# A hybrid attention and DeltaNet layer: the first triangular solve moved from VectorE to GpSimd, its closing operations pinned, and four more PSUM banks for the convolutions ahead of it

## The chip, the cores and the metric

The kernel runs on one core of a Trainium2 chip. The core has TensorE (PE, matmuls; PEld is its weight load), VectorE (DVE), ScalarE (ACT), GpSimd (POOL) and SyncE (SP, which here issues the DMAs). Each engine works off its own queue in order, and they wait for one another by semaphores. The metric is the device time of one execution in microseconds, the median of several.

## What is computed

One layer on 512 latent tokens of width 1024, with 256 context tokens as a prefix (reference, cut):

```
hx = modulate(rms_norm(x), sh1, sc1);  hc = modulate(rms_norm(ctx), csh1, csc1)
... = split_cols(hx @ w_in),  split_cols(hc @ w_in[:, :CTX_COLS])
attn_x = latent_attention(q_x, [k_c, k_x], [v_c, v_x])       # 8 heads, 2 kv heads
q, k, v = silu(dwconv_centred(qkv, conv_w)), q and k normalised  # 8 DeltaNet heads of 128
for d in (forward, backward):                                # state of the context first, then latents
    a_mat = strict_lower(beta * dec * (k k^T)) + I           # per chunk
    u, w  = triangular_solve(a_mat, [beta v, beta exp(gam) k])
    scan over chunks: delta = u - w S;  o = q_dec S + p delta;  S = g S + k_dec^T delta
gdn_x = rms_norm(o) * silu(z)
x = x + g1 * (sigmoid(g_a) * (attn_x @ w_pa) + sigmoid(g_d) * (gdn_x @ w_pd)) @ w_out
x = x + g2 * conv_ffn(modulate(rms_norm(x), sh2, sc2))
return rms_norm(x, final_norm_w)
```

All of it is float32. Large products are done as three matmuls on a split of each operand into a high and a low part (hi and lo).

## The kernel before

The layer goes through in stages: modulation and first projections (to about 65 us), attention's projections (to about 155), attention with some DeltaNet projections woven in (to about 325), the DeltaNet part with the remaining projections woven in (to about 840), then the output projection and the MLP.

**Two streams in the DeltaNet part.** From line 1272 on, two generators are interleaved. `fill = filler()` (lines 1177 to 1246) is a fixed list of dense work in steps: projections of six more k and v heads with their convolutions, of 128 rows by 768 tokens (12 steps each); then for each of 8 heads the q projection and the z projection (8 steps each); 16 gate projections (8 steps each); the merging projection `w_pa` (64 steps) and last `w_pd` (64 steps). A step is three 512-column matmuls or six 256-column ones (`gemm_steps`, line 254, and `head_steps`, line 1248). The other stream is the DeltaNet work itself: for each of four pairs of heads (p = 0 to 3) the masks (`gdn_prep`), the solve (`gdn_solve`, `gdn_solved`), the inverse of the whole chunk (`gdn_inv`) and the scan (`gdn_scan`), with `gdn_out` for the pair before. `weave(g, rate)` (line 1275) advances `fill` by `rate` steps at each yield of g. While `pinned[0]` is set, every matmul stays in the order in which the program wrote it (line 84), so PE's order is that of the weave. The other engines' orders are chosen by a scheduler from priorities (`first`, `sooner`, `solver`, `early`) and its estimate of when inputs are ready; `keep_in_program_order` puts one instruction behind the one written just before it for the same engine.

**Where the first pair stands.** Lines 1294 to 1297: 24 fill steps (WK), then the solve of pair 0 with one fill step at each of its four yields, its closing operations `gdn_solved(pre, False)`, then 66 fill steps (W0). So 94 steps stand ahead of the first `gdn_inv`. Later pairs are solved while the pair before is inverted and scanned (`stage`, line 1298), on GpSimd (`SPOOL`, line 64), and closed inside the scan with pinned instructions (lines 1049 and 1069).

**The solve.** `gdn_solve` (line 879) makes k k^T into the bank `pk`, multiplies it into the masked decay `NN` on DVE, copies the 32 by 32 diagonal blocks into `C`, transposes to `X`, and then runs 31 rows of substitution, each a multiply (`prod`, line 910) and an add (`R`, line 912) on 31 to 256 elements a partition: 62 instructions, on the engine `eng`, which is DVE for pair 0. `gdn_solved` (line 916) scales R and transposes it into `o_tr` and `o_nt`, always on DVE. `gdn_inv` begins with matmuls on these two (bank `pb`).

**The masks of a pair.** `gdn_prep` (line 851) loads rows of decays over all partitions, once into NN and once into the buffer `Gb` (one buffer for all pairs) for each of two heads, adds a mask on an engine (DVE for pair 0 since P0 is 1, GpSimd for the rest), takes the exponential on ACT and adds the two. `decay_mask` (line 1004) does the like for the scan's masks `M`, its add on GpSimd with `msk_i` (line 159).

**Convolutions.** `conv_proj` (line 278) takes a bank for the 512 latent tokens and one for the 256 context tokens from `mbank` (line 188), which has 2 banks (`mmp`, tag `mm`; tile `mb` in the profile). `conv_taps` (line 266) reads the bank with one ACT and two DVE instructions (tile `t`), `conv_silu` (line 273) makes the output `co` with ACT and DVE. `tokens` (line 289), put off by AKP = 18 ticks (two to a 512-column product), transposes `co` on PE into the one bank `xb`; its `finish` makes two powers of six columns for each k head on GpSimd (`rkk`, `hk`, lines 317 and 320), priority `first`.

**PSUM.** The DeltaNet part has 2 banks `mb`, 1 bank `xb`, 4 banks `pb` (`gps`, line 834, taken through `pbank`) and 1 bank `pk`. The four pb banks have no user until the first `gdn_inv`.

**The tail.** After the last scan: `last = gdn_out(3)`, its first part, then RW = 10 fill steps, then per head of the pair a transpose of the output, a multiply and a split, with RO = 2 fill steps after each (lines 1316 to 1319), then all that is left of `fill`. `paired` (line 1260) does the first two column blocks of `w_pd` together, head by head; the step of a head whose input does not exist yet yields without doing anything (lines 1263 and 1264). Heads 6 and 7 are made by `gdn_out(3)`.

Of the kernel before, what the change touches and what calls it, by code (L numbers as in the profile page):

```python
# [6 lines left out]
F32 = mybir.dt.float32  # L7
# [7 lines left out]
P = 128  # L15
# [9 lines left out]
NH = 8  # L25
# [3 lines left out]
NRM = "dve"  # L29
SOLVE = 2500000  # L30
POPS = (1, 3, 5, 7)
CHUNK, WK, W0, W1, RI, RS, RO = 1, 24, 66, 0, 3.0, 2.8, 2.0
RI0 = 2.4
NB = 6 - NX
POOLW = 0
# [25 lines left out]
U0, U1 = 2, 5  # L61
RW = 10
AKP = 18
SPOOL = [int(c) for c in '123']
AP2 = 7
PIN = 1
RA = .6
# [9 lines left out]
def hybrid_layer_body(tc, x, ctxt, xT, consts, cols, rows, w_mod1, w_mod2, w_av, w_aq, w_cm, w_pa, w_pd, w_out,  # L77
# [27 lines left out]
    def tt(out, a, b, op, eng=None):  # L105
        (eng or V).tensor_tensor(out=out, in0=a, in1=b, op=op)  # L106
# [10 lines left out]
    def act(out, a, f=AF.Copy, **kw):  # L117
        A.activation(out, a, f, **kw)  # L118
# [13 lines left out]
    with es:  # L132
# [32 lines left out]
            ts(col[:, S_BMOD + o:S_BMOD + o + 8], col[:, S_BMOD + o:S_BMOD + o + 8], 1.0, ALU.add)  # L165
        mhalf = cp.tile([P, 32], F32, name="mhalf")
        V.memset(mhalf, -0.5)
        half6 = cpad[:, S_END:S_END + 6]
        G.memset(half6, 0.5)
        epss = {v: cpad[:, S_END + 6 + i:S_END + 7 + i] for i, v in enumerate((1.0, 4.0, 512.0))}  # L170
        for v, t in epss.items():
            G.memset(t, v * EPS)
        mod = cr.tile([P, 48], F32, name="mod")
# [11 lines left out]
        def transpose(out, in_):  # L185
            T.transpose(out, in_, ident)

        def mbank():
            return mmp.tile([P, 512], F32, name="mb", tag="mm")

        def m2bank():
# [36 lines left out]
        ngam = cp.tile([P, 96], F32, name="ngam")  # L228
        eg = cp.tile([P, 96], F32, name="eg")
        kdec = cp.tile([P, 96], F32, name="kdec")  # L230
        hks = [(cp if i else cr).tile([P, 6], F32, name=f"hk{i}") for i in range(NH)]
        glast = cp.tile([P, 96], F32, name="glast")
        qsc = [cp.tile([P, 8], F32, name=f"qsc{i}") for i in range(4)]
        rkk = [cp.tile([P, 6], F32, name=f"rkk{i}") for i in range(NH)]
        rkq = [cp.tile([P, 4], F32, name=f"rkq{i}") for i in range(NH)]

        hx_es = ExitStack()
# [51 lines left out]
        def tokens(h, part, src):  # L289
            n = 4 if part == 0 else 6  # L290
            if part != 2:
                kss = stp.tile([P, 6], F32, name="gkss", tag="gkss", bufs=2)
            if part != 0:
                o = cbuf()

            def piece(c0, m):
                pb = xbank()
                for i in range(m):
                    transpose(pb[:, i, :], src[:, (c0 + i) * P:(c0 + i + 1) * P])
                with first():  # L300
                    if part == 1:
                        act(o[:, c0 * P:(c0 + m) * P], flat(pb)[:, 0:m * P])
                    if part != 2:
                        for i in range(m):
                            act(pb[:, i, :], pb[:, i, :], AF.Square, accum_out=kss[:, c0 + i:c0 + i + 1])
                    if part == 2:
                        for i in range(c0, c0 + m):
                            act(o[:, i * P:(i + 1) * P], pb[:, i - c0, :], AF.Copy, scale=hks[h][:, i:i + 1])

            def finish():  # L310
                with first():
                    if part != 0:
                        SP.dma_start((None, ktd, vtd)[part][h], o)
                    if part != 2:
                        rr, q = (rkq, rkk)[part][h], (128.0, 1.0)[part]
                        act(rr, kss[:, 0:n], AF.Identity, scale=q, bias=epss[4 * q])
                        tt(rr, rr, mhalf[:, 0:n], ALU.pow, G)
                    if part == 1:
                        act(hks[h], kss[:, 0:n], AF.Identity, scale=0.25, bias=epss[1.0])
                        tt(hks[h], hks[h], half6, ALU.pow, G)  # L320

            piece(0, 4)
            if part == 0:
                finish()
            else:
                late.insert(0, (tick[0] + AP2, lambda: (piece(4, 2), finish())))
# [71 lines left out]
        def projections(i0, i1):  # L398
            for i in range(i0, i1):
                yield from head_proj(*order[i])  # L400
# [450 lines left out]
        def gdn_prep(p, eng=G):  # L851
# [13 lines left out]
            NN = gq.tile([P, 12, P], F32, name="NN", align_bytes=2048, tag="NN", bufs=2)  # L865
            for hh in range(2):
                u = slice(6 * hh, 6 * hh + 6)
                Gb = gq.tile([P, 6, P], F32, name="Gb", tag="Gb", bufs=1)
                for d, D in ((0, NN[:, u, :]), (1, Gb)):
                    r0 = d * 48 + p * 12 + hh * 6  # L870
                    SP.dma_start(D.rearrange("p a b -> p (a b)"),
                                 gamdr[r0:r0 + 6, :].rearrange("a b -> (a b)").partition_broadcast(P))
                    tt(D, D, msk_s[d].unsqueeze(1).to_broadcast([P, 6, P]), ALU.add, eng)
                    for c in range(6):
                        act(D[:, c, :], D[:, c, :], AF.Exp, scale=-1.0, bias=gam[:, r0 + c:r0 + c + 1])
                tt(NN[:, u, :], NN[:, u, :], Gb, ALU.add, eng)
# [299 lines left out]

        def filler():
            age[0] = AKP
            yield from projections(KV, 16)
            hc_es.close()  # L1180
            gpool.append(ge.enter_context(tc.tile_pool(name="gp", bufs=1, reuse_waits="tile")))
# [106 lines left out]
        def wait(n):  # L1288
            for _ in range(n):
                yield  # L1290
# [2 lines left out]
        pinned[0] = True  # L1293
        weave(wait(WK), 1.0)
        weave(gdn_solve(pre, G if 0 in SPOOL else V), RK)
        gdn_solved(pre, False)
        weave(wait(W0), 1.0)
        def stage(p, pre, nxt):
            inv = gdn_inv(p, pre)
            if nxt is not None:  # L1300
# [280 lines left out]
```

## Time and profile before

| what | us |
|---|---|
| median of 3 runs | 1266.66 |
| lowest and highest | 1260.86, 1273.11 |
| the profiled execution | 1263.61 |
| its span, first to last instruction | 1261.8 |
| mean granted TensorE clock | 0.985 |
| PE, DVE, ACT, POOL busy | 1197.7, 837.8, 614.1, 276.9 |

Lines of the profile read "engine operation out<-in": a start time in us, a duration in us, the engine, the line (often that of a helper), the operation, the tiles by the program's names and their shapes, and in brackets the idle time of the engine before it with what ended it. In the list of waits the three numbers are us in total, how often, and the longest. A row of a stretch gives its bounds, its length, then for each engine the busy us and the count of instructions, the granted clock, the share of the DMA engines and GB/s. Asked for one tile, the same row counts that tile's instructions alone.

### The profile page before, as it was taken

What the parts mean: (1) busy time and instruction counts of PE and PEld (TensorE: products, weight loads), DVE (VectorE), ACT (ScalarE), POOL (GpSimd) and SP (SyncE); (2) the same over time, 40 slices, a digit from 0 to 9 for tenths busy, and PEclk for the clock granted to TensorE, in tenths of its full rate; (3) what the DMA queues carried; (4) which work ended last, traced back from release to release, by engine and by line L of the source; (5) the groups of instructions that cost most, each with busy time, mean ns of one, the idle gap of its engine ahead of it and who ended that gap; (6) DMA issues with size and microseconds to landing.
All of it is one profiled execution on the core that took longest, in us unless ns stands there. A gap on an engine that the chain in (4) does not pass through costs nothing.

```text
span 1261.8 us, 20507 instructions
## 1 busy us (share of the span) xinstructions
PE 1197.7 (95%) x7733; PEld 1017.9 (81%) x7733; DVE 837.8 (66%) x1608; ACT 614.1 (49%) x1402; POOL 276.9 (22%) x347
## 2 busy tenths in 40 slices
PE   7999899999878999999999989899999999999997
PEld 4599889899767788778888778679988888888886
DVE  5667767777699866866657777866765566653333
ACT  6534476666766663763635532223544444442231
POOL 0030110110432496596484100220000000000000
PEclk8999999999999999999999999989999999999998
DMA  9312311121636434444436776883133332233331
GB/s 380 138 59 84 103 42 68 71 76 59 204 110 196 158 126 141 137 146 141 147 124 206 260 262 203 270 309 117 51 100 100 100 101 94 90 96 95 102 93 67
DMA packets 66323, 171.31 MB, mean 136 GB/s; under 512 B 7376, under 2 KB 18096, under 8 KB 64816
## 3 DMA queue, kind: packets, MB, share of 16 engines
q1 hardware_dynamic: 66224, 170.00, 40.4%
q8 instruction: 61, 1.00, 0.3%
q14 instruction: 38, 0.31, 0.1%
HBM read 144.75 MB, written 25.21 MB: 135 GB/s over the span
## 4 chain that ended last, share of the span: by engine, by line
PE 72%; DVE 9%; DMA 8%; POOL 4%; ACT 4%; issue 3%; SPq 0%; POOLq 0%; DVEq 0%; ACTq 0%
PE mc L85 32%; PE mb L85 17%; PE pq L85 6%; PE pb L85 5%; PE pS L85 3%; PE ab L85 3%; DMA wl<-in_w_mod_dram 2%; DVE wlo L106 2%; PE pm L85 2%; PE ab L89 2%; DMA Gb<-gamdr 1%; POOL prod L106 1%; POOL R L106 1%; POOL NN L106 1%; PE pk L85 1%
## 5 line engine op out<-in xcount | busy, mean ns | idle before, releaser
L106 DVE TENSOR_TENSOR wlo<-wraw,whi 128x1024 fp32r<-128x1024 f32 (+1 forms) x153 | 192.7, 1260 | 159.1 <-ACT whi L118 158.2
L118 ACT ACTIVATE whi<-wraw 128x1024 fp32r<-128x1024 f32 (+1 forms) x153 | 159.7, 1044 | 215.0 <-PE mc L85 109.0
L85 PE MATMUL mc<-h,whi 128*128 128x512 f32 (+1 forms) x752 | 219.7, 376 | 0.3 <-ACT whi L118 0.3
L85 PE MATMUL mb<-hxH,whi 128*128 128x512 f32 x384 | 161.4, 420 | 5.4 <-DVE t L115 2.7
L85 PEld LDWEIGHTS mc<-h,whi 128*128 128x128 f32 x752 | 138.0, 188 | 26.1 <-ACT whi L118 0.5
L85 PE MATMUL mb<-hxH,wlo 128*128 128x512 f32 x384 | 151.3, 394 | 0.0
L85 PE MATMUL mb<-hxL,whi 128*128 128x512 f32 x384 | 150.8, 393 | 0.0
L85 PE MATMUL mc<-h,wlo 128*128 128x512 f32 (+1 forms) x376 | 141.3, 376 | 0.5 <-DVE wlo L106 0.5
L85 PE MATMUL mc<-a,whi 128*128 128x512 f32 (+1 forms) x396 | 111.1, 366 | 0.6 <-DVE x L115 0.6
L106 POOL TENSOR_TENSOR rc<-rc,mhalf 128x2 f32<-128x2 f32 x4 | 3.0, 745 | 411.5 <-DVE rc L112 411.5
L85 PEld LDWEIGHTS mb<-hxH,wlo 128*128 128x128 f32 x384 | 72.5, 189 | 16.6
L85 PEld LDWEIGHTS mb<-hxH,whi 128*128 128x128 f32 x384 | 72.9, 190 | 15.8 <-issue 3.6
L85 PEld LDWEIGHTS mc<-a,whi 128*128 128x128 f32 x396 | 71.5, 189 | 12.8 <-DVE x L115 0.8
L85 PEld LDWEIGHTS mc<-h,wlo 128*128 128x128 f32 x376 | 70.8, 188 | 13.6 <-DVE wlo L106 1.0
L85 PEld LDWEIGHTS mb<-hxL,whi 128*128 128x128 f32 x384 | 73.1, 190 | 9.6
L85 PE MATMUL mc<-a,wlo 128*128 128x512 f32 (+1 forms) x198 | 72.3, 365 | 0.0
L115 DVE SCALAR_TENSOR_TENSOR u<-mc,col,u 128x511 f32<-128x511 f32 x88 | 65.3, 746 | 1.4
L106 POOL TENSOR_TENSOR R<-R,prod 128x31 f32<-128x31 f32 (+15 forms) x93 | 58.1, 625 | 7.0
L106 POOL TENSOR_TENSOR prod<-X,R 128x31 f32<-128x31 f32 (+15 forms) x93 | 53.3, 573 | 19.9 <-DVE X L106 13.2
L85 PE MATMUL pq<-whi,hxH 128*128 128x256 f32 (+1 forms) x192 | 55.4, 288 | 0.0
L85 PE MATMUL pq<-wlo,hxH 128*128 128x256 f32 (+1 forms) x192 | 54.1, 282 | 0.0
L85 PE MATMUL pq<-whi,hxL 128*128 128x256 f32 (+1 forms) x192 | 54.0, 281 | 0.0
(323 smaller groups left out, 2768.5 us busy)
## 6 DMA issues: line engine op xcount, KB each, us to landing
wraw<-in_w_cm_dram SPq DMA_DIRECT2D x48, 512.0 KB, 3.5
wraw<-in_w_up_dram SPq DMA_DIRECT2D x44, 512.0 KB, 3.3
wl<-in_w_mod_dram SPq DMA_DIRECT2D x32, 512.0 KB, 4.6
wm<-in_w_mod_dram SPq DMA_DIRECT2D x8, 1024.0 KB, 10.3
wraw<-in_w_down_dram SPq DMA_DIRECT2D x16, 512.0 KB, 3.5
wraw<-in_w_aq_dram SPq DMA_DIRECT2D x10, 512.0 KB, 4.2
M<-gamdr SPq DMA_DIRECT2D x64, 64.0 KB, 4.8
wraw<-in_w_pa_dram SPq DMA_DIRECT2D x8, 512.0 KB, 4.6
```

What stands on the lines that cost most here:

```text
L85: i = nc.tensor.matmul(*a, **k)
L89: i = nc.tensor.transpose(*a, **k)
L106: (eng or V).tensor_tensor(out=out, in0=a, in1=b, op=op)
L115: V.scalar_tensor_tensor(out=out, in0=a, scalar=s, in1=b, op0=op0, op1=op1)
L118: A.activation(out, a, f, **kw)
```

## The change

- The first solve runs on GpSimd (`SPOOL` gains 0). Its closing operations are pinned in DVE's queue (`gdn_solved(pre, True)`) and stand later in the program: after 74 fill steps, with 8 more steps (WC) between them and the first inversion. Ahead of that inversion stand 24 + 4 + 66 + 8 + 8 = 110 fill steps instead of 94.
- The first 94 fill steps take their banks for projections from the four pb banks; then `mbank` goes back to its own two.
- The scan's mask is copied on GpSimd into a new tile, pinned behind the solve's last instruction, and `decay_mask` reads the copy.
- Pair 0's second decay buffer comes from the ring `q4` (three buffers), so it is no longer shared with the other pairs.
- The two powers of a k head become one of twelve columns, and all powers in `tokens` get a higher priority.

```diff
-CHUNK, WK, W0, W1, RI, RS, RO = 1, 24, 66, 0, 3.0, 2.8, 2.0
+CHUNK, WK, W0, W1, RI, RS, RO = 1, 24, 74, 0, 3.0, 2.8, 2.0
+WC = 8
...
-SPOOL = [int(c) for c in '123']
+SPOOL = [int(c) for c in '0123']
...
-        half6 = cpad[:, S_END:S_END + 6]
-        G.memset(half6, 0.5)
-        epss = {v: cpad[:, S_END + 6 + i:S_END + 7 + i] for i, v in enumerate((1.0, 4.0, 512.0))}
+        half12 = cpad[:, S_END:S_END + 12]
+        G.memset(half12[:, 0:6], -0.5)
+        G.memset(half12[:, 6:12], 0.5)
+        epss = {v: cpad[:, S_END + 12 + i:S_END + 13 + i] for i, v in enumerate((1.0, 4.0, 512.0))}
...
+        spare = []
+
         def mbank():
+            if spare:
+                return flat(spare[0].tile([P, 4, P], F32, name="pb", tag="pb"))
             return mmp.tile([P, 512], F32, name="mb", tag="mm")
...
-        hks = [(cp if i else cr).tile([P, 6], F32, name=f"hk{i}") for i in range(NH)]
+        rks = [cp.tile([P, 12], F32, name=f"rk{i}") for i in range(NH)]
+        rkk, hks = [r[:, 0:6] for r in rks], [r[:, 6:12] for r in rks]
...
-        rkk = [cp.tile([P, 6], F32, name=f"rkk{i}") for i in range(NH)]
...
                         act(rr, kss[:, 0:n], AF.Identity, scale=q, bias=epss[4 * q])
-                        tt(rr, rr, mhalf[:, 0:n], ALU.pow, G)
-                    if part == 1:
-                        act(hks[h], kss[:, 0:n], AF.Identity, scale=0.25, bias=epss[1.0])
-                        tt(hks[h], hks[h], half6, ALU.pow, G)
+                        if part == 1:
+                            act(hks[h], kss[:, 0:n], AF.Identity, scale=0.25, bias=epss[1.0])
+                        with sooner():
+                            if part == 1:
+                                tt(rks[h], rks[h], half12, ALU.pow, G)
+                            else:
+                                tt(rr, rr, mhalf[:, 0:n], ALU.pow, G)
...
-                Gb = gq.tile([P, 6, P], F32, name="Gb", tag="Gb", bufs=1)
+                Gb = (gq.tile([P, 6, P], F32, name="Gb", tag="Gb", bufs=1) if p else
+                      flat(gq.tile([P, 32, 32], F32, name="Gq", align_bytes=2048, tag="q4", bufs=3))[:, 0:768].rearrange("p (a b) -> p a b", b=P))
...
             age[0] = AKP
+            spare.append(gps)
...
         weave(gdn_solve(pre, G if 0 in SPOOL else V), RK)
-        gdn_solved(pre, False)
-        weave(wait(W0), 1.0)
+
+        msk = gq.tile([P, 2, P], F32, name="msk")
+        tc.keep_in_program_order(G.tensor_copy(out=msk, in_=cst[:, C_MI:C_MI + 256].rearrange("p (a b) -> p a b", b=P)))
+        msk_i = (msk[:, 0, :], msk[:, 1, :])
+        weave(wait(W0 - WC), 1.0)
+        spare.clear()
+        weave(wait(WC), 1.0)
+        gdn_solved(pre, True)
+        weave(wait(WC), 1.0)
```

## The prediction

> **What bounds the kernel now.** I read the first table of the page, then the busy times of two stretches, then who TensorE waited for in each.
>
> ```profile
> span 1261.8 us, 20507 instructions
> ...
> PE 1197.7 (95%) x7733; PEld 1017.9 (81%) x7733; DVE 837.8 (66%) x1608; ACT 614.1 (49%) x1402; POOL 276.9 (22%) x347
> ```
>
> TensorE (PE) is busy 1197.7 of 1261.8 us, so what any edit can win is some of the 64 us in which it stands still. The change keeps every matmul; it moves waits. Two stretches matter: the one in which the first solve runs, and the tail after the last scan.
>
> ```profile
> 325.00:420.00 95.00, 78.98 (x529) 66.80 (x528) 80.97 (x165) 66.88 (x188) 38.85 (x32) 0.99 0.52 171
> 782.00:842.00 60.00, 53.79 (x233) 41.77 (x232) 48.70 (x74) 18.09 (x35) 16.66 (x9) 0.99 0.81 272
> ```
>
> The columns are the stretch, its length, busy us of PE, PEld, DVE, ACT and POOL, then granted clock, DMA share and GB/s. In the first stretch PE stands still for 95 - 79.0 = 16.0 us, VectorE (DVE) is busy 81 of 95 us, GpSimd (POOL) 39. Whom PE waited for there:
>
> ```profile
> PE xb L89 <- DVE co L115: 4.8, 3, 1.9
> PE mb L85 <- DVE t L115: 2.7, 3, 1.7
> PE mb L85 <- DVE R L106: 2.7, 1, 2.7
> PE xb L89 <- ACT co L118: 1.6, 1, 1.6
> PE pb L85 <- DVE gT L864: 1.6, 1, 1.6
> PE pk L85 <- DVE NN L106: 1.4, 2, 1.1
> PE pb L85 <- DVE o_tr L926: 1.3, 1, 1.3
> ```
>
> These rows add up to 16.1 us, so they are the whole idle time. `mb` is the start of a convolution's projection that finds both banks still being read by DVE; `xb` is a transpose that waits for a finished convolution; `pk` waits for the masked decay NN; `pb` is the first inversion, which waits for the closing operations of the solve.
>
> **The change part by part.** *The solve leaves DVE.*
>
> ```profile
> 363.30:412.20 48.90, 27.24 (x62) 0.00 (x0) 1.00 0.54 176
> ```
>
> These are the solve's 62 instructions alone: 27.24 us of DVE time, stretched over 48.9 us because other DVE work is let in between. On POOL the same 62, as the next and the last solve show (second number: POOL):
>
> ```profile
> 445.60:495.70 50.10, 0.00 (x0) 37.36 (x62) 1.00 0.38 124
> 626.90:668.20 41.30, 0.00 (x0) 36.44 (x62) 1.00 0.41 142
> ```
>
> It takes 41.3 us with nothing between and 50.1 us with masks and powers between. So POOL is slower an instruction (36.9/27.2 = 1.35) but about as fast from end to end. The Trainium skill's GPSIMD Engine Reference, section 4.1 Engine selection, says to do elementwise work on VectorE because GpSimd is about twice as slow with two inputs; by that factor this solve would be busy 54 us, end some 18 us later than I put it, and the gain at the closing would be gone. The traced 1.35 speaks against the factor here.
>
> What lies inside the moved solve: the power operations of two or three heads.
>
> ```profile
> L106 POOL TENSOR_TENSOR M<-M,cst 128x256 f32<-128x256 f32 x32 | 28.3, 894 | 49.7 <-DMA M<-gamdr 40.0 <-DVE R L921 6.4 <-PE mb L85 2.7
> ...
> L106 POOL TENSOR_TENSOR rkk<-rkk,mhalf 128x6 f32<-128x6 f32 x8 | 12.5, 1558 | 166.4 <-ACT rkk L118 166.4
> ```
>
> Two 6-column powers (rkk, hk) become one of 12 columns. No row has 12 columns; it lies between one of 6 columns, 1.56 us, and two, 3.1 us. I take 2.3 (the middle), three times: 7 us. The eight scan masks M of pair 0 (8 x 0.89 = 7.1 us) now come behind the solve, through the copied mask, whose 256 columns I price as one such M row, below 0.9 us. They are used in the first scan, after the inversion, so they cost nothing; if that cover were gone, 7 us. The masks of pair 1 now come ahead of the solve, since the buffer Gb is pair 1's alone from the start. POOL's 39 + 36 us in that stretch, of about 92, still fit.
>
> The solve's input is ready at about 363 now. Pair 0's two Gb buffers come from the q4 ring and are loaded one right behind the other, where now the second waits for the first to be consumed; with the pk waits (1.4 us) gone too I take 360 (bounds 352 and 363). Then R is done at 360 + 41.3 + 7 = 408.
>
> *The closing operations.*
>
> ```profile
> 412.12 1.23 DVE L921 TENSOR_TENSOR R<-R,gT 128x1024 f32<-128x1024 f32 x1
> 413.38 1.95 DVE L926 STREAM_TRANSPOSE o_tr<-R 128x1024 f32<-128x1024 f32 x1
> 415.19 1.95 DVE L926 STREAM_TRANSPOSE o_nt<-R 128x1024 f32<-128x1024 f32 x1
> ```
>
> They take 5.0 us from 412.1 to 417.1. o_tr ends at 415.3 and PE waited 1.3 us for it, so PE arrived at 414.0. In the change PE has 16 more fill steps to do before it arrives (24 + 4 + 66 = 94 steps become 24 + 4 + 66 + 8 + 8 = 110), and the closing is pinned in DVE's queue 8 steps ahead of that. A fill step is three 512-column matmuls, 0.69 us (the rows at 785.06 and 785.74 below), so 16 are 11.0 us. With 8.5 us of waits removed before it (next paragraph), PE arrives at 414.0 + 11.0 - 8.5 = 416.5 and the closing ends at 408 + 5.0 = 413.4: hidden, with 3 us to spare. Behind the pinned instruction wait the taps and silu of the projections that follow; PE has their banks to wait for. Gain 2.9 (1.6 + 1.3), bounds 0 and 2.9.
>
> *The banks and the relieved DVE.* Four pb banks serve the convolutions for the first 94 steps. A projection with context takes two, so a full head of slack comes in. The mb rows go: 2.7 + 2.7 = 5.4. The pk row goes with the earlier Gb: 1.4. The xb rows (6.4) wait for a chain ACT, DVE, ACT, DVE and not for a bank:
>
> ```profile
> 383.89 0.66 PE L89 MATMUL xb<-cst,co 128*128 128x128 f32 x4 [1.87 <-DVE co L115]
> ...
> 407.67 0.44 PE L89 MATMUL xb<-cst,co 128*128 128x128 f32 x2 [1.58 <-ACT co L118]
> ```
>
> These two (3.45) fall in or right behind the solve, and a DVE with 27 us less to do shortens that chain; the others fall where ACT works off mask exponentials, which stay. I take half, 1.7. Bounds for all xb: a gain of 6.4, or a loss of 5.4 if PE, no longer held by banks, runs into them instead. Together 8.5.
>
> *The clock.*
>
> ```profile
> 416.00:418.00 2.00, 0.81 (x78) 0.81 (x82) 2.00 (x3) 1.60 (x5) 1.89 (x3) 0.91 0.04 15
> 418.00:420.00 2.00, 2.00 (x41) 1.94 (x32) 1.94 (x4) 1.91 (x7) 1.86 (x4) 0.50 0.36 53
> 420.00:422.00 2.00, 2.00 (x9) 1.69 (x8) 0.75 (x2) 0.67 (x4) 1.82 (x4) 0.73 0.90 322
> ```
>
> Right behind the wait at the closing the granted clock is 0.91, 0.50 and 0.73: (0.09 + 0.50 + 0.27) x 2 us = 1.7 us lost. Without the wait that goes: 1.7 more. The front gives 8.5 + 2.9 + 1.7 = 13.1 us (bounds 4.3, which is pk and closing alone, and 17.8, all of it).
>
> *The tail.* This is what speaks against the change. All of the fill work is a fixed list; 16 steps done early are missing later. The last 64 steps (merging projection w_pd) go head by head, and the step of head 6 yields empty until the last output stage has made it.
>
> ```profile
> 777.79 1.05 PE L85 MATMUL pb<-S,qT 128*128 128x128 f32 x8
> ...
> 785.06 0.62 PE L85 MATMUL mb<-g_s,whi 128*128 128x512 f32 x2
> 785.74 0.62 PE L85 MATMUL mb<-g_s,whi 128*128 128x512 f32 x2
> ...
> 789.87 0.60 PE L89 MATMUL pb<-cst,oacc 128*128 128x128 f32 x4
> ...
> 796.31 0.40 PE L85 MATMUL mb<-g_k,wlo 128*128 128x512 f32 x1
> ```
>
> ```profile
> 778.12 0.75 DVE L1066 COPY dl<-pb 128x256 f32<-128x256 f32 x2
> ...
> 788.96 1.66 DVE L110 TENSOR_SCALAR oacc<-oacc,f 128x128 f32<-128x128 f32 x8
> ```
>
> Between the last scan's readout (ends 778.6) and the end of the paired w_pd steps (796.7) lie 18.1 us, in which PE does 20 steps: 3 in the scan, 10 in the fixed wait RW, and the rest around the transposes. The transposes at 789.87 start when DVE has scaled the first head (rows from 788.96), so now the 10 steps just cover a chain of DVE, ACT, POOL and DVE. Sixteen steps ahead, only 4 steps (heads 6 and 7) are left for these 18 us. The chain stays; it can start earlier only by the 3 steps that stood before its matmuls, bounded by dl (done at 778.9 instead of 780.8): 0 to 1.9, and the splits of the last two heads are then exposed. I take 0.8 shorter: loss 11.0 - 0.8 = 10.2 (bounds 9.1 and 11.0). PE then idles some 7 us in one piece. After the shorter wait above the clock fell, so I add the same 1.7 here (bounds 0 and 3.5). The Trainium skill, TensorE: Matmul & The Clock Gate, Part 1, says that an idle window of about 3.4 us halves the clock and as long a busy one restores it; by it the sum would be this 1.7 as well, but charged on matmuls that wait anyway, so nearer 0.
>
> During that idle time weights and gates keep arriving, and the steps behind have waits of their own:
>
> ```profile
> PE mb L85 <- DVE gd L115: 3.3, 3, 2.1
> PE mc L85 <- DVE y L115: 2.4, 2, 1.6
> ```
>
> 5.7 us, with DMA at a share of 0.81. Double buffers let little run ahead: I take 1.0 back (bounds 0 and 5.7).
>
> *Sum.* -13.1 + 10.2 + 1.7 - 1.0 = -2.2 us. The profiled execution took 1263.61 us (span 1261.8, 1.8 around it), so 1261.4, told as 1261. That execution lies 3 us under the median of the three runs (1266.66).
>
> **The rivals.** (1) *The front gives everything and the tail is made good*: all 16.1 and the clock 1.7, a loss of 10.2, 5.7 taken back: 1263.6 - 13.3 = 1250. For it: DMA is the busy part of the tail, and it gets 10 us of free time. Against: loads wait for two buffers each. (2) *The solve ends late, slower than before*: place, DVE's queue at step 102. If R is later than 411, the pinned closing ends behind PE's 416.5, and DVE, holding taps and silu, waits with it. The 50.1 us of solve 1 from 363 would do it (413, closing over at 418). Closing 2.9 and clock 1.7 are not won, and DVE is held about 2 us, which comes back at banks: 1263.6 - 8.5 + 10.2 + 1.7 - 1.0 + 2.0 = 1268. (3) *The banks don't do what they say*: the mb waits turn into xb waits, as the chain through ACT and DVE is the true limit; 5.4 and 1.7 are not won: 1261.4 + 7.1 = 1268.5. For it: xb already waits longer than mb. Against: in that stretch DVE loses a third of its work. The Trainium skill's factor of two belongs to (2); the traced ratio bears it out little.
>
> **How the numbers follow.** Forecast 0.48 (own range 1256 to 1266), rival 1 0.22, rival 2 0.17, rival 3 0.13. The extremes of the bounds are 1263.6 - 17.8 + 9.1 - 5.7 = 1249 and 1263.6 - 4.3 + 11.0 + 3.5 = 1274; the range 1250 to 1272 holds the forecast, most of the rivals, and leaves out the ends. Against the median of before, 1% is 1254 and 1279; 1% is about what a measurement of this kernel can tell from no change. Under 1254 come two thirds of rival 1, and a little of the forecast: 0.16. Over 1279 only if rivals 2 and 3 come together with the full loss in the tail: 0.09. Within: 0.75.
>
> **What would show it.** Right: no mb wait before 420; the 62 solve instructions on POOL, ending before 411; the first pb wait gone, the clock at 1.0 there; PE idle in the 325 to 420 part near 3 to 5 us; and in the tail one idle piece of about 7 us before the transposes of the last pair, with about 11 us of new idle time in all. Wrong: if no step is missing in the tail, the time falls to about 1250; if xb waits grow by the size of the mb waits, or the first inversion waits for R, it is rival 3 or 2. A stretch 420 to 780 that idles more than now by over 3 us would be something I have not priced.

## The result and the profile after

The changed kernel takes 1298.37 us (median of 4 runs, 1297.74 to 1299.34), the kernel before 1264.72: a ratio of 1.0257 (95% interval 1.0232 to 1.0282). It is 2.6% slower; the prediction was 1261, with a range of 1250 to 1272. The first table of the page of the profiled execution (1298.55 us):

```profile
span 1296.7 us, 20486 instructions
...
PE 1215.6 (94%) x7733; PEld 1024.5 (79%) x7733; DVE 819.4 (63%) x1546; ACT 613.3 (47%) x1402; POOL 314.0 (24%) x403
```

Two things are in these lines. TensorE stands still for 1296.7 - 1215.6 = 81.1 us, 17.0 more than before. And the same 7733 matmuls are busy 17.9 us longer: about half of the loss is not waiting but slower matmuls. VectorE lost the 62 solve instructions and 18 us of work, and nothing came of it.

Line numbers have moved by one in the helpers (matmul L86, transpose L90) and by eleven in the closing operations (L932, L937). Two rows of the time line cut the execution in three, the first inversion and the first step of the output projection. Before, then after:

```profile
415.39 0.24 PE L85 MATMUL pb<-o_tr,NN 32*32 32x32 f32 x2 [1.33 <-DVE o_tr L926]
...
833.70 0.63 PE L85 MATMUL mc<-y,whi 128*128 128x512 f32 x2
```

```profile
436.21 0.26 PE L86 MATMUL pb<-o_tr,NN 32*32 32x32 f32 x1
...
857.91 0.63 PE L86 MATMUL mc<-y,whi 128*128 128x512 f32 x2
```

| stretch | before | after | difference | without the 16 moved steps (11.0 us) | predicted |
|---|---|---|---|---|---|
| start to first inversion | 415.4 | 436.2 | +20.8 | +9.8 | -13.1 |
| first inversion to output projection | 418.3 | 421.7 | +3.4 | +14.4 | +10.9 |
| output projection to end | 428.1 | 438.8 | +10.7 | +10.7 | 0 |
| span | 1261.8 | 1296.7 | +34.9 | +34.9 | -2.2 |

**The front.** Whom TensorE waited for between 330 and 437 (in all, times, longest):

```profile
PE xb L90 <- DVE co L116: 17.8, 5, 8.4
PE xb L90 <- ACT co L119: 1.3, 1, 1.3
PE pk L86 <- DVE NN L107: 1.2, 2, 1.0
```

The mb rows of before (5.4) and both pb rows (2.9) are gone, as predicted. But the xb rows, waits of a transpose for a finished convolution, grew from 6.4 to 19.1: in all 20.3 where 16.1 stood before. The longest one is at the pinned closing. The solve on GpSimd, first and last instruction and what stood ahead of it:

```profile
340.57 2.51 POOL L107 TENSOR_TENSOR NN<-NN,cst 128x768 f32<-128x768 f32 x1 [11.83 <-DMA NN<-gamdr]
...
348.01 2.28 POOL L107 TENSOR_TENSOR rk<-rk,col 128x12 f32<-128x12 f32 x1
...
369.03 0.24 POOL L107 TENSOR_TENSOR prod<-X,R 128x31 f32<-128x31 f32 x1 [1.52 <-DVE X L107]
...
418.16 0.25 POOL L107 TENSOR_TENSOR R<-R,prod 128x31 f32<-128x31 f32 x1
```

It runs from 369.0 to 418.4, not from 360 to 408. What that does on VectorE, and then on TensorE:

```profile
350.32 1.87 DVE L116 SCALAR_TENSOR_TENSOR g<-beta,rk 128x6 f32<-128x6 f32 x2 [2.50 <-POOL rk L107]
...
360.23 2.05 DVE L116 SCALAR_TENSOR_TENSOR co<-co,t 128x768 f32<-128x768 f32 x1 [2.22 <-ACT co L119]
...
412.09 0.67 DVE L116 SCALAR_TENSOR_TENSOR co<-tz,pb 128x512 f32<-128x512 f32 x1
418.44 1.39 DVE L932 TENSOR_TENSOR R<-R,gT 128x1024 f32<-128x1024 f32 x1 [5.68 <-POOL R L107]
419.86 2.13 DVE L937 STREAM_TRANSPOSE o_tr<-R 128x1024 f32<-128x1024 f32 x1
421.81 2.20 DVE L937 STREAM_TRANSPOSE o_nt<-R 128x1024 f32<-128x1024 f32 x1
...
427.32 0.16 DVE L107 TENSOR_TENSOR f<-rkq 128x4 f32<-128x4 f32 x1 [0.93 <-POOL rkq L107]
...
430.30 1.35 DVE L107 TENSOR_TENSOR wlo<-wraw,whi 128x1024 fp32r<-128x1024 f32 x1 [2.16 <-ACT whi L119]
431.57 0.98 DVE L116 SCALAR_TENSOR_TENSOR co<-co,t 128x512 f32<-128x512 f32 x1
```

```profile
432.61 1.12 PE L90 MATMUL xb<-cst,co 128*128 128x128 f32 x4 [8.42 <-DVE co L116]
```

VectorE is free at 412.8, stands 5.7 us in front of the closing, works 5.6 us on it, and only then makes the taps and the silu (co, 431.57) for which TensorE has been waiting 8.4 us. On the way it stands twice more: 0.9 us for a power that GpSimd makes behind the eight mask additions of the first scan (418.8 to 426.3), and 2.2 us for ScalarE, which does ten exponentials for these masks (3.1 us, from 425.2) ahead of the split of weights (whi) and the silu. No run takes these two apart from the late closing. The wait before the first inversion is gone only because it now stands one step ahead of it. Behind it the granted clock is 0.63:

```profile
426.00:440.00 14.00, 7.39 (x120) 6.09 (x121) 5.86 (x9) 7.96 (x24) 7.85 (x12) 0.63 0.45 151
```

**The tail** is as predicted in kind: one long wait ahead of the last transposes, then two more, and the clock of the whole piece at 0.52 (second fence; the same piece of before, 788 to 802, had PE busy 12.84 of 14 us).

```profile
808.40 1.11 PE L90 MATMUL pb<-cst,oacc 128*128 128x128 f32 x4 [5.64 <-DVE oacc L111]
811.10 0.80 PE L86 MATMUL mb<-g_k,whi 128*128 128x512 f32 x1 [1.58 <-ACT g_k L119]
816.68 0.80 PE L86 MATMUL mb<-g_k,whi 128*128 128x512 f32 x1 [1.50 <-ACT g_k L119]
```

```profile
806.00:820.00 14.00, 8.51 (x21) 5.74 (x22) 6.64 (x19) 2.79 (x4) 2.16 (x2) 0.52 0.04 6
```

**The output projection and the MLP**, which the diff does not touch. One hundred microseconds of each kernel, before and then after:

```profile
1000.00:1100.00 100.00, 100.00 (x443) 82.81 (x442) 61.77 (x75) 42.57 (x55) 0.00 (x0) 1.00 0.30 98
```

```profile
1000.00:1100.00 100.00, 100.00 (x431) 80.65 (x430) 59.16 (x72) 42.45 (x54) 0.00 (x0) 1.00 0.29 95
```

TensorE is busy for all of it at full clock in both, but does 431 matmuls in place of 443: 232 ns from one start to the next (the pitch) and not 225.7, 2.8% more. Over the 428 us of the table's third row that would be 11.9 us if all matmuls there were like these; the row has 10.7.

### The profile page after: what moved, and what is told of

Read it like the earlier page. It is cut to its first block, busy times and chain, and to the rows that moved or that the text cites. A ratio compares the mean times of both kernels' runs of the same rounds, so it can differ in the third digit from the quotient of the medians.

```text
span 1296.7 us, 20486 instructions
## 1 busy us (share of the span) xinstructions
PE 1215.6 (94%) x7733; PEld 1024.5 (79%) x7733; DVE 819.4 (63%) x1546; ACT 613.3 (47%) x1402; POOL 314.0 (24%) x403
## 5 line engine op out<-in xcount | busy, mean ns | idle before, releaser
L86 PE MATMUL mc<-h,whi 128*128 128x512 f32 (+1 forms) x752 | 223.9, 382 | 0.3 <-ACT whi L119 0.3
L86 PEld LDWEIGHTS mc<-h,whi 128*128 128x128 f32 x752 | 138.1, 188 | 30.0 <-ACT whi L119 0.5
L86 PE MATMUL mc<-h,wlo 128*128 128x512 f32 (+1 forms) x376 | 143.5, 382 | 0.5 <-DVE wlo L107 0.5
L86 PE MATMUL mb<-hxH,whi 128*128 128x512 f32 x312 | 131.6, 422 | 0.0
L86 PE MATMUL mb<-hxH,wlo 128*128 128x512 f32 x312 | 123.6, 396 | 0.0
L86 PE MATMUL mb<-hxL,whi 128*128 128x512 f32 x312 | 122.8, 394 | 0.0
L86 PE MATMUL mc<-a,whi 128*128 128x512 f32 (+1 forms) x396 | 113.0, 371 | 0.6 <-DVE x L116 0.6
L86 PEld LDWEIGHTS mc<-a,whi 128*128 128x128 f32 x396 | 71.5, 188 | 14.8 <-DVE x L116 0.8
L86 PEld LDWEIGHTS mc<-h,wlo 128*128 128x128 f32 x376 | 70.8, 188 | 15.7 <-DVE wlo L107 1.0
L107 POOL TENSOR_TENSOR prod<-X,R 128x31 f32<-128x31 f32 (+15 forms) x124 | 75.0, 605 | 23.7 <-DVE X L107 14.6
L107 POOL TENSOR_TENSOR R<-R,prod 128x31 f32<-128x31 f32 (+15 forms) x124 | 78.2, 630 | 9.3
L86 PE MATMUL mc<-a,wlo 128*128 128x512 f32 (+1 forms) x198 | 73.4, 371 | 0.0
L86 PEld LDWEIGHTS mb<-hxH,wlo 128*128 128x128 f32 x312 | 59.0, 189 | 13.3
L86 PEld LDWEIGHTS mb<-hxL,whi 128*128 128x128 f32 x312 | 59.6, 191 | 7.4
L86 PEld LDWEIGHTS mb<-hxH,whi 128*128 128x128 f32 x312 | 59.5, 191 | 7.4
L107 POOL TENSOR_TENSOR rk<-rk,col 128x12 f32<-128x12 f32 x8 | 20.6, 2572 | 152.6 <-ACT rk L119 152.6
L86 PE MATMUL pq<-whi,hxH 128*128 128x256 f32 (+1 forms) x192 | 55.4, 288 | 0.0
L86 PE MATMUL pq<-wlo,hxH 128*128 128x256 f32 (+1 forms) x192 | 54.1, 282 | 0.1
```

The lines of the kernel that those rows point to most:

```text
L86: i = nc.tensor.matmul(*a, **k)
```

## The experiments

All ratios are to the kernel before, timed on the same chip, with 95% intervals; a ratio can differ by a few tenths of a per cent from that of the medians. Three questions: what slows matmuls that nobody touched, what the 16 moved steps cost, and what the front lost.

**The address.** The diff takes one tile of 24 bytes (hk0) out of the pool `cr` and makes the tiles of the key norms in `cp` 32 bytes longer in all. By the compiled programs' address lists hxH and hxL lie 32 bytes higher after it, and so does every weight tile (the first whi at 29152, not 29120); the data of the output projection and the MLP (y2, h2, a2) are aligned to 512 bytes and do not follow. Theory A: this is the 2.8%. Theory B: something that the new order of work leaves behind.

*e1_after_layout*: the kernel after, tiles back at the old addresses.

```diff
-        mhalf = cp.tile([P, 32], F32, name="mhalf")
+        mhalf = cp.tile([P, 24], F32, name="mhalf")
...
+        pad = cr.tile([P, 8], F32, name="pad")
+        V.memset(pad, 0.0)
```

> The kernel after, with every weight tile and every tile of the output projection and the MLP back at the SBUF address that it had before (32 bytes lower); nothing else differs. Theory A (the 32 bytes slow the matmuls that read these tiles): the stretch from the first mc step to the end falls from 431.9 us to about 422 (421.9 before), the mean of one 512-column matmul there from 232 to 226 ns, and the whole by 8 to 11 us, to 1287 to 1290. Theory B (the last stretch is slow for another reason: what the solve on GpSimd left behind in the queues, or the clock): no change, 1297 to 1299.

1286.97 us, 1.0184 (1.0156 to 1.0212): 11.4 us less than after by the medians, 9 by the ratios. In its profile the stretch from the output projection to the end is 428.8 us long, 10.0 shorter than after. The window:

```profile
1000.00:1100.00 100.00, 100.00 (x443) 82.81 (x442) 60.28 (x73) 43.88 (x56) 0.00 (x0) 1.00 0.28 95
```

*e2_before_shift*: the kernel before, tiles 32 bytes higher.

```diff
-        hks = [(cp if i else cr).tile([P, 6], F32, name=f"hk{i}") for i in range(NH)]
+        hks = [cp.tile([P, 6], F32, name=f"hk{i}") for i in range(NH)]
```

> The kernel before, with the same tiles moved up by 32 bytes, to the addresses that they have after; nothing else differs. Theory A (the address): 8 to 11 us slower than before, about 1274, all of it behind the first mc step. Theory B (not the address): 1263 to 1266, as before.

1271.66 us, 1.0085 (1.0054 to 1.0115): 11 us slower by the ratio, 7 by the medians (1264.65 before). There are 431 matmuls in the window, and the last stretch is 8.9 us longer. Theory B falls: the address alone takes and gives some 10 us. Which address, the next three show: weights alone up by 32 (mhalf 40 columns long), hxH and hxL alone up by 32 (hk0 into cp, mhalf 24), weights alone up by 64 (mhalf 48).

> The kernel before with a longer table of constants, which moves the weight tiles up by 32 bytes (the first from 29120 to 29152) and leaves hxH, the other operand of the projections, where it was. Theory A1 (the address of the weights counts): 225.7 ns for a 512-column matmul become 232, all 11 us of the second experiment are lost, about 1275. Theory A2 (the address of the other operand counts): before's time, 1262 to 1267.

1277.2 us, 1.0099 (1.0065 to 1.0134).

> The counterpart: the kernel before with hxH, the constants of the transposes and the gates' tiles 32 bytes higher, while the weight tiles of the MLP keep their address. A1: before's time, 1262 to 1267, and 225.7 ns in the MLP. A2: part of the 11 us is lost ahead of the output projection.

1268.54 us, 1.0026 (1.0008 to 1.0045).

> The kernel before with the weight tiles 64 bytes higher (the first at 29184, a multiple of 512). If only a multiple of 64 bytes is asked for: 225.7 ns and before's time, 1262 to 1267. If a larger step counts: the pitch falls towards 213 to 220 ns and the time by 10 to 30 us.

1274.33 us, 1.0072 (1.0047 to 1.0097). The MLP window of e10, e11 and e12, in this order:

```profile
1000.00:1100.00 100.00, 100.00 (x430) 80.53 (x429) 59.12 (x72) 42.47 (x54) 0.00 (x0) 1.00 0.28 95
```

```profile
1000.00:1100.00 100.00, 100.00 (x443) 82.81 (x442) 60.01 (x73) 43.44 (x56) 0.00 (x0) 1.00 0.28 99
```

```profile
1000.00:1100.00 100.00, 100.00 (x430) 80.59 (x429) 59.11 (x72) 42.37 (x54) 0.00 (x0) 1.00 0.27 95
```

In the MLP the weights count, and 64 bytes hurt as much as 32. In the projections, which read hxH, six successive triples of matmuls tell the pitch (first and last row of the six); before, and then e11:

```profile
325.48 0.39 PE L85 MATMUL mb<-hxH,wlo 128*128 128x512 f32 x1
...
328.92 0.40 PE L85 MATMUL mb<-hxH,wlo 128*128 128x512 f32 x1
```

```profile
329.82 0.40 PE L85 MATMUL mb<-hxH,wlo 128*128 128x512 f32 x1
...
333.33 0.40 PE L85 MATMUL mb<-hxH,wlo 128*128 128x512 f32 x1
```

Between these rows lie 15 matmuls: 3.44 / 15 = 229 ns before, 3.51 / 15 = 234 in e11 (hxH moved) and 233 in e10 (weights moved), but 230 in e2, where both moved together. So it is the distance between the two operands, not either address (weights 64 bytes higher, 3.40 / 15 = 227 ns in e12, is good here). That accounts for e10 = e2 + e11 within their intervals. The last two change the distance from the other side: hxH and hxL 64 bytes lower, and the data of the MLP 256 bytes higher.

```diff
+        pad = cr.tile([P, 16], F32, name="pad")
+        V.memset(pad, 0.0)
```

> The kernel before with hxH and hxL 64 bytes lower, so that weights (29120) and hxH (192448) are a multiple of 512 bytes apart; weights and MLP tiles stay. If the distance between the two operands sets the pitch: the projections run at 228 ns as in the kernel with the weights 64 bytes higher (229.5 before, 233 at a distance that is 32 off), the MLP keeps 225.7, and 1 to 3 us come off, about 1261. If the address of each tile by itself counts: no change, or slower.

1264.77 us, 1.0000 (0.9980 to 1.0019): no gain in time. The pitch did move as expected: over all projections of 512 columns that follow one another without a gap between 325 and 425 us (some 130 matmuls a kernel) it is 228.0 ns here and 228.1 in e12, which have the same distance, and 229.3 before.

```diff
-            t = pool.tile([P, 2 * k * NL + 64], F32R, align_bytes=512, name=name)
+            t = pool.tile([P, 2 * k * NL + 128], F32R, align_bytes=512, name=name)
...
-            h2H, h2L = two(h2p, KT, 192, "h2")
+            h2H, h2L = two(h2p, KT, 448, "h2")
```

> The kernel before with the data of the output projection and the MLP 256 bytes further inside their tiles, so that weights and data are a multiple of 512 apart there (256 off before). If a multiple of 256 is all that counts: 225.7 ns and before's time, 1262 to 1267. If 512 is better: below 225.7 ns and faster, 5 us for each 2.6 ns. If 512 is worse: towards 232, up to 10 slower.

1265.81 us, 0.9998 (0.9981 to 1.0016), 443 matmuls in the window. In the MLP 225.7 ns hold at a distance of 0 and of 256 bytes (modulo 512), 232 ns at 32 or 64 beside 256. Before had the good distance already, so there is nothing to win here. That the distance counts, and not the address of the weights alone, is shown in the projections; in the MLP the data were moved by 256 bytes only, which does not separate the two. Why the distance counts no run shows.

**The 16 steps.**

*e4_before_late* and *e13_before_74*: the kernel before with 82 and with 74 steps ahead of the first inversion (the diff for 82).

```diff
-CHUNK, WK, W0, W1, RI, RS, RO = 1, 24, 66, 0, 3.0, 2.8, 2.0
+CHUNK, WK, W0, W1, RI, RS, RO = 1, 24, 82, 0, 3.0, 2.8, 2.0
```

> The kernel before, with 82 steps ahead of the first inversion in place of 66: solve on VectorE, masks, banks and unpinned closing as before. It prices the tail. The prediction's terms: 10.2 for the uncovered transposes, 1.7 clock, 1.0 back, less the wait for the closing that the 16 steps now cover (2.9 and 1.7 of clock): 6 us slower, about 1270. What the kernel after shows of that stretch (15 us lost between the first inversion and the first mc step): 15.1 less 4.6, 10 to 11 slower, about 1275. If the loss there belongs to the solve on GpSimd and not to the 16 steps: under 3 slower.

1285.51 us, 1.0169 (1.0134 to 1.0205): 21 us, twice what I had from the trace. Its tail has the same wait to the hundredth as the kernel after:

```profile
804.01 1.12 PE L89 MATMUL pb<-cst,oacc 128*128 128x128 f32 x4 [5.64 <-DVE oacc L110]
```

In the profiled execution, the fastest of four (1279.25), the stretch from the first inversion to the output projection loses 10.7 us, the predicted size. From the end of attention to the inversion it loses 5.4 us more than the 16 steps, at a granted clock of 0.94 from 325 to 437 (0.98 before). The three other executions took 5 to 9 us more; what they lost and where was not traced.

> The kernel before with 74 steps ahead of the first inversion: half of the shift of the fourth experiment (82 steps, 1285.5). If each step that leaves the tail costs the same: half of its 20.9, 1275. If there are steps to spare in the tail up to a point: 1265 to 1268 (the first wait for the closing, 2.9, goes too). If the first steps cost most (the cover is already too short now): 1279 to 1284.

1270.18 us, 1.0039 (1.0020 to 1.0057), 5 us: the first eight steps cost little, the second eight 16.

*e14_before_58*: the same constant at 58.

> The kernel before with 58 steps ahead of the first inversion: 8 fewer. With 74 it cost 5, with 82 it cost 21. If the tail still gains from more steps: the wait for the closing grows by 5.5 and the tail gives 5 or more back, 1260 to 1267. If 66 already covers the tail: 5 to 8 slower, 1270 to 1273.

1277.58 us, 1.0103 (1.0072 to 1.0135), 13 us. The closing's wait grew by 5.8 us, as the row shows, and the tail gave nothing back: the stretch from the first inversion to the output projection is 12.0 us longer, of which the 8 steps are only 5.5. So the 66 of before is the best of the four tried.

```profile
418.63 0.31 PE L85 MATMUL pb<-o_tr,NN 32*32 32x32 f32 x2 [7.15 <-DVE o_tr L926]
```

*e5_after_94*: the kernel after with the old addresses (so have all later variants of the kernel after), and W0 = 58, that is 66 steps between solve and inversion as before.

> The kernel after with the old addresses (as in the first experiment), and with the 16 steps back behind the first inversion: 66 steps between solve and inversion in place of 82; solve on GpSimd, pinned closing, masks, banks as after. Theory A (the first four runs add up: layout 11, the 16 steps 20, banks 1.6, the rest nothing): 20 us faster than with the 82 steps, about 1267. Theory C (the solve on GpSimd ends at 418 and the first inversion waits for it): the tail's 11 to 14 come back, but PE stands some 9 to 13 us ahead of the first inversion, so 1275 to 1285.

1270.41 us, 1.0067 (1.0042 to 1.0093). In the changed kernel the 16 steps cost 1.0184 - 1.0067, about 15 us. The expected 13 us of waiting for the late solve are 5.9 (below), so most of theory A and a part of theory C hold.

**The front.** What e5 leaves of the change, 0.67%, stands ahead of the first inversion: that comes 6.6 us later than before in its profile (421.95 for 415.39), and the rest of the kernel loses nothing. That execution was the fastest of its six.

*e3_before_banks*: the spare banks alone, in the kernel before.

```diff
+        spare = []
+
         def mbank():
+            if spare:
+                return flat(spare[0].tile([P, 4, P], F32, name="pb", tag="pb"))
...
+            spare.append(gps)
...
-        weave(wait(W0), 1.0)
+        weave(wait(W0 - 8), 1.0)
+        spare.clear()
+        weave(wait(8), 1.0)
```

> The kernel before, with the four spare PSUM banks for the convolutions alone: solve, masks, closing and the 66 steps as before. The prediction's own terms: the mb waits go (5.4) and the clock keeps up (up to 1.7): 5 to 7 us faster, about 1258. Rival 3 (the waits turn into xb waits, since the chain through ACT and DVE sets the pace): within 1.5 us of before. Theory A does not depend on it: no change behind 420 us.

1266.28 us, 1.0026 (1.0006 to 1.0045): no gain. Its waits up to the first inversion:

```profile
PE xb L89 <- DVE co L115: 9.5, 4, 3.6
PE pb L85 <- DVE o_tr L930: 3.7, 1, 3.7
PE xb L89 <- ACT co L118: 1.8, 1, 1.8
PE pb L85 <- DVE gT L868: 1.5, 1, 1.5
```

*e16_after_94_nobanks*: e5 without the spare banks (`spare.append(gps)` left out).

> The fifth experiment (old addresses, 66 steps, solve on GpSimd) without the spare banks. If the banks let TensorE run ahead into one long wait that halves the clock: the xb wait of 4.9 us at 346 shrinks to 1.8 to 2.9 with mb waits of 5 in its place, the clock stays up there, and 2 to 4 us come off, about 1272 by this chip's before. If banks help here as the prediction had it: 5 to 7 slower, about 1277.

1268.25 us, 1.0041 (1.0022 to 1.0059). The waits of e5 (with banks) and then e16 (without):

```profile
PE xb L90 <- DVE co L116: 9.4, 4, 4.9
PE pb L86 <- DVE o_tr L939: 5.9, 1, 5.9
...
PE xb L90 <- ACT co L119: 1.2, 1, 1.2
```

```profile
PE mb L86 <- DVE t L116: 3.8, 3, 3.3
PE xb L90 <- DVE co L116: 3.0, 2, 1.7
PE mb L86 <- DVE g L107: 2.5, 1, 2.5
PE xb L90 <- ACT co L119: 1.7, 2, 0.9
```

With banks 10.6 us of xb and no mb; without 4.7 of xb and 6.3 of mb, 11.0 together. The banks turn one wait into the other and win nothing, and they gather it in longer pieces. In e3 a single wait of 3.0 us, which ends at 386, has this around it (granted clock 0.66; 1.00 in the 10 us ahead):

```profile
383.00:393.00 10.00, 6.99 (x32) 6.46 (x31) 7.55 (x20) 5.91 (x17) 1.87 (x2) 0.66 0.12 45
```

*e8_after_dve* (82 steps) and *e15_after_94_dve* (66 steps): the first solve back on VectorE.

```diff
-SPOOL = [int(c) for c in '0123']
+SPOOL = [int(c) for c in '123']
```

> The kernel after with the old addresses, and with the first solve back on VectorE (82 steps, banks, pinned closing, masks as after). Theory A (the move of the solve is worth nothing by itself): 1284 to 1289, as the first experiment. Theory C (the late solve on GpSimd costs the front): the closing is over before the inversion, the xb wait of 8.4 us goes, 8 to 10 faster, about 1278. The prediction's view (VectorE's 62 solve steps delay the convolutions): 4 to 7 slower than the first experiment, about 1292.

1280.16 us, 1.0143 (1.0107 to 1.0179): 0.4 points, about 5 us, better than e1. The intervals overlap, but the traces have the same sign. Counted from one VectorE instruction at the start of the DeltaNet part (the scaling gwh, at 325.2 in before and after), the first inversion comes after 104.8 us, and after 109.9 to 112.1 in the four kernels with 82 steps and the solve on GpSimd (after, e1, e6, e9). The xb wait of 8.4 us at the closing is gone, although the closing begins at 416.1, hardly before the 418.4 of the kernel after: with the solve in its own queue VectorE does the convolutions' work between the solve's instructions and does not stand. The earlier xb waits stay (5.5, 3.6 and 2.2 us). The prediction's view had the opposite sign.

> The kernel after with the old addresses, the 16 steps behind the inversion again, and the first solve back on VectorE: left of the change are banks, masks, merged powers and the pinned closing. If the solve on GpSimd costs its 5 to 7 with 66 steps too: 1264 to 1267. If banks and masks cost the 8.5 that the fifth experiment left: 1270 to 1273.

1268.62 us, 1.0040 (1.0020 to 1.0060), 0.27 points better than e5. The intervals overlap.

*e6_after_powers* (two powers of 6 columns again) and *e9_after_unpinned* (`gdn_solved(pre, False)`), both with 82 steps.

> The kernel after with the old addresses, and with the powers of the key norms as before: two of 6 columns in place of one of 12, in their old place in the order. Theory A: no change against the first experiment (1287). Theory C (R is late because a 12-column power stands ahead of VectorE's g and of two sweeps of the solve): the solve ends 3 to 6 us earlier, the wait of 8.4 us ahead of the first inversion shrinks by as much, 1281 to 1284.

1286.56 us, 1.0191 (1.0156 to 1.0226): no change. The solve begins and ends where it did; VectorE stands 1.6 us for the powers and then 2.9 for k k^T from TensorE.

> The kernel after with the old addresses, and with the closing operations not pinned into the order, so that the scheduler places them where it likes. Theory A: no change, 1284 to 1289. Theory C (the pinned closing holds VectorE 5.7 us and its convolutions 5 us more while R is late): the xb wait of 8.4 us shrinks to 2 to 4, and 4 to 6 us come off, about 1282.

1286.76 us, 1.0193 (1.0156 to 1.0230): no change; the closing stands in the same place of VectorE's queue, with the same stand of 5.7 us ahead of it. So pinning it does nothing here; that it waits in that queue, which e8 ends, does.

*e7b_after_94_gb*: e5 with pair 0's decay tile back in its one buffer.

```diff
-                Gb = (gq.tile([P, 6, P], F32, name="Gb", tag="Gb", bufs=1) if p else
-                      flat(gq.tile([P, 32, 32], F32, name="Gq", align_bytes=2048, tag="q4", bufs=3))[:, 0:768].rearrange("p (a b) -> p a b", b=P))
+                Gb = gq.tile([P, 6, P], F32, name="Gb", tag="Gb", bufs=1)
```

> The fifth experiment with pair 0's second decay tile back in its single shared buffer, so that the second half's masks wait for the first's. If the masks done ahead (ScalarE's 24 exponentials back to back, GpSimd's adds beside VectorE's taps) make the xb wait of 4.9 us: it falls to 2 to 3.5 and the solve starts within 2 us of now; up to 3 us faster. If they only start the solve earlier: the solve starts 3 to 5 us later and the wait ahead of the first inversion grows by as much, about 1276.

1269.2 us, 1.0036 (1.0010 to 1.0061). TensorE now runs ahead and waits for the solve:

```profile
424.05 0.31 PE L86 MATMUL pb<-o_tr,NN 32*32 32x32 f32 x2 [12.44 <-DVE o_tr L938]
```

The longest early xb wait falls from 4.9 to 3.85 us, and TensorE is ready for the inversion at 411.6 in place of 416.1 (421.95 - 5.87), while the solve's result comes 2 us later. So the masks done ahead hold up the convolutions; without them the end of the solve decides. They also hold up the solve itself, which was not expected: without the extra buffer it starts at 364.66, 4.3 us earlier than in e5 (368.97).

```profile
364.66 0.24 POOL L107 TENSOR_TENSOR prod<-X,R 128x31 f32<-128x31 f32 x1 [1.22 <-DVE X L107]
```

It ends later mainly because three additions of later pairs' masks (5.9 us) now stand between its instructions on GpSimd.

Each of banks, GpSimd solve and masks, taken back alone, wins a quarter to a third of a per cent from the 0.67; the intervals overlap with e5's, so how the 0.67 is shared stays open. No version beat the kernel before. Of the parts only the banks were run alone in it (e3), and they won nothing.

| part | cost, per cent | from |
|---|---|---|
| address of the weights | 0.73 | after - e1 (e2 alone: 0.85) |
| 16 steps ahead | 1.17 | e1 - e5 (e4 alone: 1.69) |
| GpSimd solve, banks, masks | 0.67 | e5 |
| all | 2.57 | after |

## Why the prediction was wrong

Forecast was a front that wins 13.1 us, a tail that loses 10.9, and nothing elsewhere. The tail was right, the front failed, and a third term was missing. The missing term alone does not explain the miss: at the old addresses (e1) the change still takes 1287 us, above the range, and the tail has its forecast size there, so it is the front that failed.

1. *"R is done at 360 + 41.3 + 7 = 408"* failed first. The length came out near (48.3 predicted, 49.4 measured), the start did not: 369.0. I let the second decay tile and the missing pk wait pull the start ahead by 3 us, and the extra buffer puts it back instead: by e7b the solve starts 4.3 us earlier without it. With it pair 1's masks run ahead of the solve, as the prediction said, but at a price that it left out. GpSimd does three of them, of 2.5 us each, in a row (340.57 to 348.0), then a 12-column power of 2.28 us, and VectorE stands 2.5 us for that power before it goes on to the decay products that the solve needs. Behind the products it stands 2.2 us more (360.23) for a convolution's silu, which ScalarE made behind exponentials of pair 1's masks, and copies the diagonal blocks from 362.2 (354.1 before). The power was priced right (2.3), but not who stands behind it; two short ones in its place change nothing (e6). Two more powers lie among the solve's instructions, and VectorE stands 4.8 and 3.6 us for them: with the 2.5 that is 10.9 us, where it stood 0.4 before.

That the length came out near is luck, since two misses cancel. There are two powers in it and not three (4.6 us for 7), and the 62 instructions are busy longer than the 36.4 us of the solve that gave the 41.3, and than the mean of 36.9:

```profile
369.00:418.50 49.50, 40.35 (x62) 1.00 0.56 188
```

40.35, which is 1.48 of VectorE's 27.24. The Trainium skill, GPSIMD Engine Reference, section 4.1, says about two; this case lies between it and the 1.35 that I took.

2. *"Hidden, with 3 us to spare"* fell with it. This is rival 2, at the place that it named: R later than 411, VectorE held in front of the pinned closing. Its price was 2 us of held queue; it is 5.7 us of standing and an xb wait of 8.4, because the convolution that TensorE needed next stood right behind. That wait goes when the solve goes back to VectorE (e8). The scan's masks, which were to *"cost nothing"*, stand in the way of the same convolution on GpSimd and ScalarE.

3. *"The mb rows go: 5.4"* was right in the trace and wrong as a gain. This is rival 3: e5 against e16 has 10.6 us of waiting with banks and 11.0 without. *"A DVE with 27 us less to do shortens that chain"*, 1.7, had the wrong sign: from 325 to 420 VectorE fell from 81.0 to 56.0 busy us, and xb rose. What holds its chain is the order in the queues and not VectorE's share of busy time.

```profile
325.00:420.00 95.00, 82.63 (x451) 69.88 (x450) 55.96 (x99) 58.98 (x168) 67.93 (x79) 0.98 0.54 178
```

Rivals 2 and 3 were held to be alternatives with chances of 0.17 and 0.13, and a time over 1279, which needed both and the full loss in the tail, got 0.09. They came together; both go with a VectorE queue that is late. The front's lower bound, 4.3, was also tighter than its own terms: with the closing at 0 and xb at its loss of 5.4 they give 1.4. The front as measured, a loss of 9.8, lies far below both.

4. *The tail* was right in mechanism and near in size: 14.4 in the profile after and 11.5 in e1, where the matmuls have their old pitch, for 10.9. The clock term of 1.7 was too small: the granted clock is 0.52 for 14 us around the wait. In part TensorE waits in that time anyway. By whole executions the 16 steps cost more, 15 us (e1 against e5) and 21 (e4), and for e4 only a part of that was traced.

5. *The clock* was put at one piece of 1.7 us, won in the front and lost in the tail. The mean granted clock fell from 0.985 to 0.974, so 0.015 x 1261.8 = 19 us of full clock were withheld before and 0.026 x 1296.7 = 34 after. Of the 17.9 us by which TensorE's busy time grew, e1 takes away 8.2 (1207.4 us busy) with the address; the other 10 fit these 15, a part of which falls into waits.

6. *Nothing was priced behind the output projection.* A few small tiles in the diff moved all weights by 32 bytes, and that cost some 10 us, as much as the largest terms of the sum. No row of the profile of before could give a price for it, but the prediction could have named that the diff moves every later tile.

## What to carry to other kernels

Before moving work off a busy engine, ask what that engine's queue will stand in front of: here a queue that did the late work itself, with other work in between, lost less than one that stood waiting for the neighbour to finish it. The extra banks and the extra buffer did not help, since they removed a wait that came back one step later in the same chain; so add up all the waits of the stretch before and after. And when an edit adds, drops or resizes a small tile, compare the pitch of untouched matmuls first: it says within one window whether the layout is being timed along with the idea.

## What the runs showed of the hardware

Where a matmul's two operands lie in SBUF changes its pitch by 2 to 3 per cent: 225.7 against 232 ns for 512 columns in the MLP, 229 against 233 in the projections, for 32 bytes. In the projections it is the distance between them that counts.

The granted clock falls after waits of 3 us and less, in pieces of 3.4 us or multiples of it (by the record of the clock in the traces of before and after: 3.4, 6.8, 10.2 and 13.7). The Trainium skill, TensorE: Matmul & The Clock Gate, Part 1, gives a free-running window of about 3.4 us, and that the loss varies from run to run with its phase; the pieces agree with it. A whole 3.4 us of idle time is not needed: in e3 the half clock begins at 385.3, when TensorE has stood still for 2.2 us of its wait of 3.0, and lasts 6.8 us. Most executions of the kernel before lie between 1257.4 and 1273.1 us, so a single profile is no measure for a term of 3 us.
